# Positions loaded first, Pool's angle table ahead of the padding's memsets, powers between its steps, longer counted times for Pool

## Chip, core and metric

The kernel runs on one core of one Trainium2 chip. The time is device microseconds (us) of one execution. The core has a matrix engine (PE in the profile; its weight loads are PEld), a vector engine (DVE), a scalar engine (ACT), GpSimd (POOL) and a queue engine (SP) that issues DMA transfers; POOL can issue DMA transfers too, on a queue of its own. Each engine works off its own instructions in the order in which they were recorded, and waits where one of them needs what another engine or a transfer has not yet delivered.

## The reference

A two-layer decoder on 256 tokens of 1024 channels. Layer 0 has stick-breaking heads beside differential attention heads, layer 1 causal attention with 16 heads. The change concerns the way from the first norm to the rotated queries and keys:

```python
def rms_norm(x, g):
    y = xf * lax.rsqrt(jnp.mean(xf * xf, axis=-1, keepdims=True) + NORM_EPS)
    return y * g
def rope_tables(positions, head_dim):
    ang = positions.astype(jnp.float32)[..., None] * inv_freq     # (1, 256, 8)
    return jnp.cos(ang), jnp.sin(ang)
def apply_partial_rope(x, cos, sin):                              # of 64 channels of a head, 16 are turned
    r = jnp.concatenate([x1 * c - x2 * s, x1 * s + x2 * c], axis=-1)
# per layer:  h += mixer(rms_norm(h));  h += relu(rms_norm(h) @ w1)**2 @ w2
#             h += sigmoid(rms_norm(h) @ gate) * (p @ proj);        at the end rms_norm(h)
```

## The kernel before

All matrix products of the weights are made in three passes: a weight tile of 512 KB lands in one of four `raw` buffers, ACT rounds it to `whi`, DVE makes the rest `wlo = raw - whi`, and PE multiplies `whi` by the activations' high and low parts (`T0h`, `T0l`) and `wlo` by the high part (L159). Six pairs `whi`/`wlo` are in flight. In layer 0 the column blocks come in the order `bq`, `bk` (the differential heads' queries and keys), `aq`, `ak`, `av`, `bv`.

The order of instructions on each engine is made by a planner when the program is built (class `Order`). Tasks are generators; each yields the time or the event for which it waits, and of those that can go on the one of lowest rank goes on. `spend` adds a counted cost in ns to an engine's clock. The counted costs decide nothing on the chip but the order in which instructions stand. `o.idle(engine)` lets a task wait until the planner's clock of that engine has come by.

What the change touches:

- `table_task` makes the cosines and sines. POOL casts the positions (`posi` to `posf`), multiplies by the frequencies (`ang`) and takes multiples of 2 pi off in small steps (`prod`, `rem`; 16 elements a partition), ACT takes the sines, DVE makes `cc` and `sn`.
- `statistics` makes a norm's factor: ACT sums squares, DVE makes `ms_a`, POOL raises it to the power -0.5 (`rs_a`, L534), DVE makes an eighth of it for the queries (`rs8`, a part of the tile `rs_a`). There are two token tiles t, so two powers.
- `rows_task` has PE spread the two factors over a row (L159 `bank<-ident,rs_a`).
- `qk_sink` takes a finished block of queries or keys out of PSUM to `tok`, scaled, has POOL turn it by `cc` and `sn` (four instructions through `tt_pool`, L196: `rp`, `rp` twice, `tok`), and has PE transpose it (L170 `bank<-ident,tok`).
- `z_tile` has POOL write zeros into the halves of `z` and `zl` that pad the keys. `ple_projection` copies its products from PSUM to `pp`.

Of the kernel before, what the change touches and what calls it, by code (L numbers as in the profile page):

```python
# [9 lines left out]
F32 = mybir.dt.float32  # L10
F32R = mybir.dt.float32r
BF16 = mybir.dt.bfloat16
I32 = mybir.dt.int32
AF = mybir.ActivationFunctionType
ALU = mybir.AluOpType
AX = mybir.AxisListType

P = 128
# [22 lines left out]
def width(ap):  # L41
    n = 1
    for s in ap.shape[1:]:
        n *= int(s)
    return n
# [37 lines left out]
class Order:  # L83
# [110 lines left out]

    def tt_pool(self, out, a, b, op, dep=0.0):
        self.nc.gpsimd.tensor_tensor(out, a, b, op=op)  # L196
        return self.spend("pool", 145.0 + 2.15 * width(out), dep)

    def stt(self, out, a, s, b, op0, op1, dep=0.0):
        dep = max(dep, self.after(out, a, s, b))  # L200
# [27 lines left out]
def kernel(  # L228
# [6 lines left out]
    nc = tc.nc  # L235
    cst = ctx.enter_context(tc.tile_pool(name="cst", bufs=1))
# [5 lines left out]
    o = Order(nc)  # L242
# [18 lines left out]
    grow = big.take()  # L261
    grow_a, grow_b = grow[1][0:16, 0:P], grow[1][0:32, P:2 * P]
    nc.gpsimd.dma_start(grow_a, attn_norm.rearrange("i (k q) -> (i k) q", q=P))
    nc.scalar.preload_act_table_set("trig_and_small")
    o.spend("act", 1300)

    def load_x(t, cs=(0, 1)):
        for c in cs:
            nc.sync.dma_start(h[t][:, c * HALF:(c + 1) * HALF], x[0, t * P:(t + 1) * P, c * HALF:(c + 1) * HALF])
            o.clk["dma"] += 730  # L270
            x_ev[t][c].t = o.clk["dma"] + 1400
# [8 lines left out]
    one = cst.tile([P, 1], F32, name="one")  # L280
    nc.vector.memset(one, 1.0)
    junk = cst.tile([P, HALF], BF16, name="junk")
    posi = cst.tile([P, 2], I32, name="posi")
    lraw = [outs.take() for _ in range(4)]
    gsub = cst.tile([P, P], F32, name="gsub")
    invf = cst.tile([P, 8], F32, name="invf")
# [99 lines left out]
    def dma_task():  # L386
        for n, u in enumerate(units):
            if n == 2:
                load_x(1)
                nc.sync.dma_start(posi, positions[0].rearrange("(t q) -> q t", q=P))  # L390
            if n == 7:
                small_loads()
            yield lambda: None if not raws.free else 0.0
            t0 = min(f[0] for f in raws.free)
            u.raw = raws.take()
            s = max(o.clk["dma"], t0, o.now + 100)
            if n == 0:
                for a in range(2):
                    nc.sync.dma_start(u.raw[1][:, a * 512:(a + 1) * 512], u.src[:, a, :])
                    s = o.clk["dma"] = max(o.clk["dma"], s) + 730  # L400
                    u.raw_ev[a].t = s + 1300
                    if a == 0:
                        load_x(0, (1,))
                        s = o.clk["dma"]
            else:
                nc.sync.dma_start(u.raw[1].rearrange("q (a n) -> q a n", a=u.a), u.src)
                u.raw_ev[0].t = u.raw_ev[1].t = s + 1430 + 1300
                o.clk["dma"] = s + 1430
# [42 lines left out]
    def drop(u):  # L451
        splits.give(*u.buf, o.clk["pe"] + o.LAT)
        used[0] += 1
# [91 lines left out]
    def mm3(ps, ahi, alo, whi, wlo, start, stop):  # L545
        o.mm(ps, ahi, whi, start, False)
        o.mm(ps, ahi, wlo, False, False)
        return o.mm(ps, alo, whi, False, stop)
# [377 lines left out]
    def ple_projection(i, pT, pT_ev, st_ev, pps, pp_ev):  # L926
        yield st_ev
        pp = vpool.tile([P, 2, D], F32, tag="s", name=f"pp{i}")
        pps.append(pp)
        us = [units[pp_at[i]], units[pp_at[i] + 1]]  # L930
        w = 0.0
        for t in range(2):
            ts_ = slice(t * P, (t + 1) * P)
            for c in range(2):
                cs = slice(c * HALF, (c + 1) * HALF)
                bk = None
                for k in range(2):
                    yield (o.idle("pe"), us[k].ev[c], pT_ev)
                    if bk is None:
                        yield banks.wake  # L940
                        bk = banks.take()
                    mm3(bk[1], pT[:, 0, k, ts_], pT[:, 1, k, ts_], us[k].hi[:, 0, cs], us[k].lo[:, 0, cs], k == 0, k == 1)

                def evac(bk, t, cs, dep):
                    yield dep
                    e = o.copy(pp[:, t, cs], bk[1], ps=True)
                    banks.give(*bk, e)
                o.add(evac(bk, t, cs, o.clk["pe"] + o.LAT), 25)
        for u in us:
            drop(u)  # L950
        pp_ev.t = o.now
# [128 lines left out]


    def table_task():
        yield 9500.0
        posf = cst.tile([P, 2], F32, name="posf")
        ang = cst.tile([P, 2, 8], F32, name="ang")
        ka = cst.tile([P, 2, 8], F32, name="ka")
        kb = cst.tile([P, 2, 8], F32, name="kb")
        rem = cst.tile([P, 2, 8], F32, name="rem")
        aux = cst.tile([P, 2, 8], F32, name="aux")
        sh = cst.tile([P, 2, 8], F32, name="sh")  # L1090
        ch = cst.tile([P, 2, 8], F32, name="ch")
        for j in range(8):
            nc.gpsimd.memset(invf[:, j:j + 1], INV_FREQ[j])
        nc.gpsimd.tensor_copy(posf, posi)
        for t in range(2):
            nc.gpsimd.tensor_tensor(ang[:, t, :], invf, posf[:, t:t + 1].to_broadcast([P, 8]), op=ALU.mult)

        magic, inv, b14 = 1.5 * 2.0 ** 23, 1.0 / (2.0 * math.pi), 2.0 ** 14
        pt = two_pi_parts()
        prod = cst.tile([P, 2, 8], F32, name="prod")  # L1100

        def affine(dst, a, m, c):
            nc.gpsimd.tensor_scalar(dst, a, m, c, op0=ALU.mult, op1=ALU.add)

        def less(dst, k, c, src):
            nc.gpsimd.tensor_scalar(prod, k, -c, None, op0=ALU.mult)  # L1106
            nc.gpsimd.tensor_tensor(dst, prod, src, op=ALU.add)  # L1107

        affine(ka, ang, inv / b14, magic)
        nc.gpsimd.tensor_scalar(ka, ka, -magic, None, op0=ALU.add)  # L1110
        less(rem, ka, pt[0] * b14, ang)
        less(rem, ka, pt[1] * b14, rem)
        less(aux, ka, pt[2] * b14, rem)
        affine(kb, aux, inv, magic)
        nc.gpsimd.tensor_scalar(kb, kb, -magic, None, op0=ALU.add)
        for k, c in ((kb, pt[0]), (ka, pt[2] * b14), (kb, pt[1]), (ka, pt[3] * b14),
                     (kb, pt[2]), (ka, pt[4] * b14), (kb, pt[3]), (kb, pt[4])):
            less(rem, k, c, rem)
        e = o.spend("pool", 8700)
        yield e  # L1120

        o.act(sh, rem, AF.Sin, scale=0.5)
        e = o.act(aux, rem, AF.Abs, scale=0.5)
        yield e
        affine(aux, aux, -1.0, math.pi / 2)
        e = o.spend("pool", 200)
        yield e
        e = o.act(ch, aux, AF.Sin)
        nc.scalar.preload_act_table_set("natural_log_exp_and_others")
        o.spend("act", 1300)  # L1130
        yield e
        for t in range(2):
            o.stt(sn[:, t, 1, :], sh[:, t, :], 2.0, ch[:, t, :], ALU.mult, ALU.mult)
            o.ts(sn[:, t, 0, :], sn[:, t, 1, :], -1.0)
            o.stt(cc[:, t, 0, :], sh[:, t, :], -2.0, sh[:, t, :], ALU.mult, ALU.mult)
            o.ts(cc[:, t, 0, :], cc[:, t, 0, :], 1.0, None, ALU.add)
            e = o.ts(cc[:, t, 1, :], cc[:, t, 0, :], 1.0)
        rope_ev.t = e

        yield (28000.0, small_ev)  # L1140
        yield o.idle("dve")
        for j in range(2):
            a, b = lraw[2 * j][1], lraw[2 * j + 1][1]
            o.tt(a, a, b, ALU.mult)
            nc.vector.tensor_reduce(lsum[:, j], a.rearrange("q (h d) -> q h d", h=4), axis=AX.X, op=ALU.add)
            e = o.spend("dve", 340)
        for l_ in lraw:
            outs.give(*l_, e)
        yield e
        e = o.act(lsum, lsum, AF.Exp)  # L1150
        yield e
        o.tt(nlam, lsum[:, 0, :], lsum[:, 1, :], ALU.subtract)
        lam_ev.t = o.ts(nlam, nlam, LAM_INIT, -1.0, ALU.add, ALU.mult)
        o.ts(gsub, gsub, 1.0 - LAM_INIT)

    o.add(table_task(), 15)

    pT = cst.tile([P, 2, 2, 256], F32R, name="pT")

# [21 lines left out]
    def z_tile(name, layer, j):  # L1181

        z = zpool.tile([P, 4, 2, 256], F32R, tag="z", name=name)
        def zeros():
            yield o.now if layer else 1500.0
            for y in (z, zl[j]) if layer == 0 else (z,):
                nc.gpsimd.memset(y[64:128, :, 0, :].bitcast(F32), 0.0)  # L1187
                nc.gpsimd.memset(y[0:64, :, 1, :].bitcast(F32), 0.0)  # L1188
                o.spend("pool", 1800)
        o.add(zeros(), 14)  # L1190
        return z, zl[j]

    sl = [cst.tile([P, 4, 256], F32R, name=f"sl{j}") for j in range(2)]
# [98 lines left out]
```

## Time and profile before

| | us |
|---|---|
| median of 3 runs | 673.91 (673.76 to 673.92) |
| the profiled execution, its own time | 674.04 |
| its span on the core | 672.2 |
| PE busy | 654.2 (97%) |
| DVE, ACT busy | 451.6, 417.2 |
| POOL busy | 62.8 (9%) |

The span runs from the first to the last instruction that the profile recorded; the execution's own time has 1.84 us around it. A matmul's recorded end is modelled, and consecutive matmuls overlap in the records, so that a wait is longer than the idle time shown.

### The profile page before, as it was taken

What the parts mean: (1) busy time and instruction counts of PE and PEld (TensorE: products, weight loads), DVE (VectorE), ACT (ScalarE), POOL (GpSimd) and SP (SyncE); (2) the same over time, 40 slices, a digit from 0 to 9 for tenths busy, and PEclk for the clock granted to TensorE, in tenths of its full rate; (3) what the DMA queues carried; (4) which work ended last, traced back from release to release, by engine and by line L of the source; (5) the groups of instructions that cost most, each with busy time, mean ns of one, the idle gap of its engine ahead of it and who ended that gap; (6) DMA issues with size and microseconds to landing.
All of it is one profiled execution on the core that took longest, in us unless ns stands there. A gap on an engine that the chain in (4) does not pass through costs nothing.

```text
span 672.2 us, 10997 instructions
## 1 busy us (share of the span) xinstructions
PE 654.2 (97%) x3906; PEld 572.0 (85%) x3906; DVE 451.6 (67%) x936; ACT 417.2 (62%) x886; POOL 62.8 (9%) x129
## 2 busy tenths in 40 slices
PE   6799999999999999999999999999999999999995
PEld 5589878899998999898887878789998999899885
DVE  6789767677457555656995776758657545655594
ACT  6667887676446544655796776758646544655482
POOL 8820001000000000000043022000000000000010
PEclk9999999999999999999999999999999999999999
DMA  7662643456476446644556434525476546654621
GB/s 256 218 205 80 188 148 103 137 172 230 147 238 214 162 154 223 220 165 147 193 198 195 136 119 151 157 95 173 154 239 217 161 147 227 220 175 144 214 95 62
DMA packets 50055, 115.61 MB, mean 172 GB/s; under 512 B 4001, under 2 KB 5457, under 8 KB 50001
## 3 DMA queue, kind: packets, MB, share of 16 engines
q1 hardware_dynamic: 49824, 114.39, 52.1%
q8 instruction: 30, 0.49, 0.3%
q0 software_dynamic: 176, 0.53, 0.2%
q14 instruction: 25, 0.20, 0.1%
HBM read 113.86 MB, written 1.05 MB: 171 GB/s over the span
## 4 chain that ended last, share of the span: by engine, by line
PE 81%; issue 8%; POOL 8%; ACT 2%; DVE 0%; POOLq 0%; DVEq 0%; ACTq 0%
PE bank L159 78%; POOL rp L196 3%; PE bank L170 2%; POOL tok L196 1%; PE bank L165 1%; ACT tok L178 1%; POOL prod L1106 1%; POOL rem L1107 1%; ACT junk L178 0%; POOL zl L1187 0%; POOL z L1188 0%; POOL zl L1188 0%; POOL z L1187 0%; ACT whi L178 0%; ACT L1028 0%
## 5 line engine op out<-in xcount | busy, mean ns | idle before, releaser
L192 DVE TENSOR_TENSOR wlo<-raw,whi 128x512 fp32r<-128x512 f32 x424 | 276.7, 695 | 87.7 <-ACT whi L178 61.9
L178 ACT ACTIVATE whi<-raw 128x512 fp32r<-128x512 f32 x424 | 243.6, 628 | 96.1 <-PE bank L159 72.0
L159 PE MATMUL bank<-T0h,whi 128*128 128x256 f32 x576 | 162.4, 282 | 0.0
L159 PE MATMUL bank<-T0h,wlo 128*128 128x256 f32 x576 | 162.0, 281 | 0.0
L159 PE MATMUL bank<-T0l,whi 128*128 128x256 f32 x576 | 162.0, 281 | 0.0
L159 PE MATMUL bank<-whi,hid 128*128 128x512 f32 x512 | 161.0, 390 | 0.0
L159 PEld LDWEIGHTS bank<-whi,hid 128*128 128x128 f32 x512 | 96.1, 188 | 19.3
L159 PEld LDWEIGHTS bank<-T0h,wlo 128*128 128x128 f32 x576 | 110.5, 192 | 0.0
L159 PEld LDWEIGHTS bank<-T0l,whi 128*128 128x128 f32 x576 | 108.3, 188 | 0.7
L159 PEld LDWEIGHTS bank<-T0h,whi 128*128 128x128 f32 x576 | 108.3, 188 | 0.7
L159 PE MATMUL bank<-wlo,hid 128*128 128x512 f32 x256 | 99.6, 389 | 0.0
L192 DVE TENSOR_TENSOR tok<-tok 128x512 f32<-128x512 f32 x32 | 22.0, 689 | 66.9 <-ACT tok L178 66.9
L159 PE MATMUL bank<-whi,T0h 128*128 128x512 f32 x160 | 65.7, 411 | 0.8 <-DVE T0h L510 0.8
L159 PE MATMUL bank<-wlo,T0h 128*128 128x512 f32 x160 | 63.4, 396 | 0.0
L178 ACT ACTIVATE tok<-bank 128x512 f32<-128x512 f32 x32 | 18.8, 587 | 71.8 <-PE bank L159 71.8
L159 PE MATMUL bank<-whi,T0l 128*128 128x512 f32 x160 | 63.1, 394 | 0.0
L159 PEld LDWEIGHTS bank<-wlo,hid 128*128 128x128 f32 x256 | 48.1, 188 | 9.3
L159 PE MATMUL bank<-whi,T1h 128*128 128x512 f32 (+1 forms) x136 | 53.4, 393 | 0.0
L159 PE MATMUL bank<-whi,T1l 128*128 128x512 f32 (+1 forms) x136 | 51.5, 379 | 0.0
L159 PE MATMUL bank<-wlo,T1h 128*128 128x512 f32 (+1 forms) x136 | 51.4, 378 | 0.0
L534 POOL TENSOR_TENSOR rs_p<-ms_p,pexp 128x1 f32<-128x1 f32 x4 | 2.2, 554 | 434.4 <-DVE ms_p L209 434.4
L159 PEld LDWEIGHTS bank<-whi,T0h 128*128 128x128 f32 x160 | 30.5, 191 | 7.0 <-DVE T0h L510 1.2
(161 smaller groups left out, 740.5 us busy)
## 6 DMA issues: line engine op xcount, KB each, us to landing
raw<-in_w_ff_dram SPq DMA_DIRECT2D x128, 512.0 KB, 4.4
raw<-in_moba_w_in_dram SPq DMA_DIRECT2D x24, 512.0 KB, 4.2
raw<-in_ab_w_in_dram SPq DMA_DIRECT2D x23, 512.0 KB, 4.3
raw<-in_ple_gate_dram SPq DMA_DIRECT2D x16, 512.0 KB, 5.0
raw<-in_ab_w_out_dram SPq DMA_DIRECT2D x8, 512.0 KB, 4.6
raw<-in_moba_w_out_dram SPq DMA_DIRECT2D x8, 512.0 KB, 3.3
raw<-in_ple_proj_dram SPq DMA_DIRECT2D x4, 512.0 KB, 3.3
h<-in_x_dram SPq DMA_DIRECT2D x4, 256.0 KB, 5.2
```

The lines of the kernel that those rows point to most:

```text
L159: self.nc.tensor.matmul(out, lhsT, rhs, start=start, stop=stop, **kw)
L165: self.nc.tensor.matmul(out, lhsT, rhs, start=start, stop=stop)
L170: self.nc.tensor.transpose(out, in_, ident)
L178: self.nc.scalar.activation(out, in_, func, **kw)
L192: self.nc.vector.tensor_tensor(out, a, b, op=op)
L196: self.nc.gpsimd.tensor_tensor(out, a, b, op=op)
L534: nc.gpsimd.tensor_tensor(nm.rs[:, t:t + 1], b, pexp[:, 0:1], op=ALU.pow)
L1106: nc.gpsimd.tensor_scalar(prod, k, -c, None, op0=ALU.mult)
L1107: nc.gpsimd.tensor_tensor(dst, prod, src, op=ALU.add)
```

## The change

The positions are loaded by POOL's queue right behind the first norm's gains, and no longer by SP behind the first weights. The angle table may start at the planner's 1.0 us where it was 9.5, and its POOL steps are put one by one, so that other POOL work can stand between them; its last POOL step goes to DVE. The padding's memsets in layer 0 wait until the planner's 18 or 30 us and stand alone as well. A POOL instruction of the rotation is counted at 565 ns whatever its width. The copies to `pp` are all ACT's.

```diff
     def tt_pool(self, out, a, b, op, dep=0.0):
         self.nc.gpsimd.tensor_tensor(out, a, b, op=op)
-        return self.spend("pool", 145.0 + 2.15 * width(out), dep)
+        return self.spend("pool", 565.0, dep)
...
     nc.gpsimd.dma_start(grow_a, attn_norm.rearrange("i (k q) -> (i k) q", q=P))
+    posi = cst.tile([P, 2], I32, name="posi")
+    nc.gpsimd.dma_start(posi, positions[0].rearrange("(t q) -> q t", q=P))
...
                 load_x(1)
-                nc.sync.dma_start(posi, positions[0].rearrange("(t q) -> q t", q=P))
...
                     yield dep
-                    e = o.copy(pp[:, t, cs], bk[1], ps=True)
+                    yield o.idle("act")
+                    e = o.act(pp[:, t, cs], bk[1], AF.Copy, ps=True)
...
     def table_task():
-        yield 9500.0
+        yield 1000.0
...
+        o.clk["pool"] = 5000.0
+
         def affine(dst, a, m, c):
             nc.gpsimd.tensor_scalar(dst, a, m, c, op0=ALU.mult, op1=ALU.add)
+            return o.spend("pool", 420)
 
         def less(dst, k, c, src):
             nc.gpsimd.tensor_scalar(prod, k, -c, None, op0=ALU.mult)
             nc.gpsimd.tensor_tensor(dst, prod, src, op=ALU.add)
...
+            return o.spend("pool", 800)
...
         for k, c in ((kb, pt[0]), (ka, pt[2] * b14), (kb, pt[1]), (ka, pt[3] * b14),
                      (kb, pt[2]), (ka, pt[4] * b14), (kb, pt[3]), (kb, pt[4])):
-            less(rem, k, c, rem)
-        e = o.spend("pool", 8700)
+            yield o.idle("pool")
+            e = less(rem, k, c, rem)
         yield e
...
-        affine(aux, aux, -1.0, math.pi / 2)
-        e = o.spend("pool", 200)
+        e = o.ts(aux, aux, -1.0, math.pi / 2, ALU.mult, ALU.add)
...
-    o.add(table_task(), 15)
+    o.add(table_task(), 32)
...
         def zeros():
-            yield o.now if layer else 1500.0
+            yield o.now if layer else (18000.0 if j else 30000.0)
             for y in (z, zl[j]) if layer == 0 else (z,):
-                nc.gpsimd.memset(y[64:128, :, 0, :].bitcast(F32), 0.0)
-                nc.gpsimd.memset(y[0:64, :, 1, :].bitcast(F32), 0.0)
-                o.spend("pool", 1800)
-        o.add(zeros(), 14)
+                for rows, g in ((slice(64, 128), 0), (slice(0, 64), 1)):
+                    yield o.idle("pool")
+                    nc.gpsimd.memset(y[rows, :, g, :].bitcast(F32), 0.0)
+                    o.spend("pool", 980)
+        o.add(zeros(), 34)
```

POOL, at the end of the angle table in layer 0, before: all eight memsets stand ahead of the table, and both powers behind its last step.

```order
L1106 TENSOR_SCALAR prod<-kb 128x16
L1107 TENSOR_TENSOR rem<-prod,rem 128x16
L534 TENSOR_TENSOR rs_a_167<-ms_a_166,pexp 128x1 x2
L1103 TENSOR_SCALAR aux<-aux 128x16
L298 CAST identb<-ident 128x128
L299 MEMSET cmask 128x256
```

The same place now (L1110 and L1111 are the table's steps, L1197 the memsets of `z` and `zl`):

```order
L1111 TENSOR_TENSOR rem<-prod,rem 128x16
L534 TENSOR_TENSOR rs_a_167<-ms_a_166,pexp 128x1
L1110 TENSOR_SCALAR prod<-kb 128x16
L1111 TENSOR_TENSOR rem<-prod,rem 128x16
L1197 MEMSET z_169 64x4x256 x2
L1197 MEMSET zl_155 64x4x256
L299 CAST identb<-ident 128x128
L300 MEMSET cmask 128x256
```

The second power stands ahead of the table's last step. The first one stands six steps from the end (of the eight in the last loop, two are done). Three memsets have come between the table and the masks; a fourth stands behind the masks, two more between the second and the third rotation, and the last two behind the fourth.

DVE in the first block of `bq` (`wlo_86` and `wlo_88` are its third and fourth weight tiles):

```order
 L527 TENSOR_REDUCE ms_a_166<-ss_a_165 128x1
 L209 TENSOR_SCALAR ms_a_166<-ms_a_166 128x1
-L192 TENSOR_TENSOR wlo_86<-raw_79,whi_85 128x512 x2
-L192 TENSOR_TENSOR wlo_88<-raw_80,whi_87 128x512 x2
+L209 TENSOR_SCALAR rs_a_167<-rs_a_167 128x1
+L192 TENSOR_TENSOR wlo_86<-raw_79,whi_85 128x512 x2
+L192 TENSOR_TENSOR wlo_88<-raw_80,whi_87 128x512 x2
```

The eighth of the first factor, which needs POOL's first power, now stands ahead of these four halves; before, nineteen further instructions stood between.

PE at the spreading of the factors, before, in the first matmuls of `bk` (`whi_89`):

```order
L159 MATMUL bank_75<-whi_87,T0l 128x512
L159 MATMUL bank_76<-whi_89,T0h 128x512
L159 MATMUL bank_76<-wlo_90,T0h 128x512
L159 MATMUL bank_76<-whi_89,T0l 128x512
L159 MATMUL bank_69<-ident,rs_a_167 128x128 x2
L159 MATMUL bank_76<-whi_89,T0h 128x512
```

And now, in the second half of `bq`:

```order
L159 MATMUL bank_75<-whi_83,T0h 128x512
L159 MATMUL bank_75<-wlo_84,T0h 128x512
L159 MATMUL bank_75<-whi_83,T0l 128x512
L159 MATMUL bank_76<-ident,rs_a_167 128x128 x2
L159 MATMUL bank_75<-whi_83,T0h 128x512
```

The spreading has moved up by 18 matmuls. The transposes of the first rotated block (`tok_100`) have gone the other way, from 15 matmuls behind that place to 45 behind it, and those of the other three blocks, and of the blocks in layer 1 too, stand some matmuls later than before.

## Rows read from the trace of the kernel before

**Rows 1.** The page: the span and the engines' busy time.
```profile
span 672.2 us, 10997 instructions
...
PE 654.2 (97%) x3906; PEld 572.0 (85%) x3906; DVE 451.6 (67%) x936; ACT 417.2 (62%) x886; POOL 62.8 (9%) x129
```

**Rows 2.** PE's timeline, layer 0: start, length, line, operation; idle before, releaser.
```profile
22.78 0.39 PE L159 MATMUL bank<-wlo,T0h 128*128 128x512 f32 x1
23.01 0.39 PE L159 MATMUL bank<-whi,T0l 128*128 128x512 f32 x1
25.02 1.01 PE L159 MATMUL bank<-ident,rs_a 128*128 128x128 f32 x4 [1.62 <-POOL rs_a L534]
25.79 0.48 PE L159 MATMUL bank<-whi,T0h 128*128 128x512 f32 x1
...
30.84 0.66 PE L170 MATMUL bank<-ident,tok 128*128 128x128 f32 x4 [1.38 <-POOL tok L196]
...
33.70 0.66 PE L170 MATMUL bank<-ident,tok 128*128 128x128 f32 x4 [0.42 <-POOL tok L196]
...
42.18 0.66 PE L170 MATMUL bank<-ident,tok 128*128 128x128 f32 x4 [0.55 <-POOL tok L196]
...
44.14 0.66 PE L170 MATMUL bank<-ident,tok 128*128 128x128 f32 x4 [0.24 <-POOL tok L196]
```

**Rows 3.** PE's timeline, layer 1, the same columns.
```profile
368.76 0.66 PE L170 MATMUL bank<-ident,tok 128*128 128x128 f32 x4 [0.35 <-POOL tok L196]
...
414.74 0.66 PE L170 MATMUL bank<-ident,tok 128*128 128x128 f32 x4 [0.36 <-POOL tok L196]
```

**Rows 4.** POOL's timeline, the same columns.
```profile
1.32 0.66 POOL L263 DMA_DIRECT2D big<-in_attn_norm_dram  x1 [0.82 <-POOLq L1278]
...
9.64 0.95 POOL L1188 MEMSET zl<- 64x1024 f32 x1
...
10.81 0.43 POOL L1094 CAST posf<-posi 128x2 f32<-128x2 int32 x1
...
19.16 0.57 POOL L1106 TENSOR_SCALAR prod<-kb 128x16 f32<-128x16 f32 x1
...
24.39 1.09 POOL L534 TENSOR_TENSOR rs_a<-ms_a,pexp 128x1 f32<-128x1 f32 x2
...
28.08 0.40 POOL L312 CAST negr<-big 128x256 fp32r<-128x256 f32 x1
...
33.18 0.46 POOL L196 TENSOR_TENSOR tok<-rp 128x128 f32<-128x128 f32 x1
```

**Rows 5.** DMA issues: transfer, queue, count, size, us from issue to landing.
```profile
gB<-in_final_norm_dram POOLq DMA_DIRECT2D x1, 512.0 KB, 3.8
...
big<-in_attn_norm_dram POOLq DMA_DIRECT2D x1, 8.0 KB, 3.3
posi<-in_positions_dram SPq DMA_DIRECT2D x1, 1.0 KB, 6.6
```

**Rows 6.** POOL's timeline at the end: the issue of the other transfer on POOL's queue.
```profile
639.51 0.67 POOL L1258 DMA_DIRECT2D gB<-in_final_norm_dram  x1
```

**Rows 7.** DVE's timeline.
```profile
9.68 1.06 DVE L510 CAST T0h<-tok 128x256 fp32r<-128x256 f32 x1
...
12.33 0.28 DVE L510 CAST T0h<-tok 128x256 fp32r<-128x256 f32 x1
...
13.50 2.54 DVE L192 TENSOR_TENSOR wlo<-raw,whi 128x512 fp32r<-128x512 f32 x4 [0.18 <-ACT whi L178]
...
25.00 0.15 DVE L209 TENSOR_SCALAR rs_a<-rs_a 128x1 f32<-128x1 f32 x1 [2.92 <-POOL rs_a L534]
```

**Rows 8.** PE's timeline: its start, and the first block of `bq`.
```profile
4.78 0.25 PE L170 MATMUL bank<-ident,big 16*128 16x16 f32 x1 [4.78 <-DMA big<-in_attn_norm_dram]
...
9.16 0.63 PE L159 MATMUL bank<-whi,T0h 128*128 128x512 f32 x1
...
14.60 0.39 PE L159 MATMUL bank<-wlo,T0h 128*128 128x512 f32 x1
```

More of the change, by code (lines that the diff above doesn't have):

```diff
@@ L282 @@
     junk = cst.tile([P, HALF], BF16, name="junk")
-    posi = cst.tile([P, 2], I32, name="posi")
     lraw = [outs.take() for _ in range(4)]
@@ L1107, in less, with whole @@
             nc.gpsimd.tensor_tensor(dst, prod, src, op=ALU.add)
[L1109 to L1115, printed above, removed]
+            return o.spend("pool", 800)
+        def whole(dst, a, m):
+            affine(dst, a, m, magic)
+            nc.gpsimd.tensor_scalar(dst, dst, -magic, None, op0=ALU.add)
+            return o.spend("pool", 420)
+        whole(ka, ang, inv / b14)
+        for d_, k, c, v in ((rem, ka, pt[0] * b14, ang), (rem, ka, pt[1] * b14, rem), (aux, ka, pt[2] * b14, rem)):
+            yield o.idle("pool")
+            less(d_, k, c, v)
+        yield o.idle("pool")
+        whole(kb, aux, inv)
         for k, c in ((kb, pt[0]), (ka, pt[2] * b14), (kb, pt[1]), (ka, pt[3] * b14),
                      (kb, pt[2]), (ka, pt[4] * b14), (kb, pt[3]), (kb, pt[4])):
-            less(rem, k, c, rem)
-        e = o.spend("pool", 8700)
+            yield o.idle("pool")
+            e = less(rem, k, c, rem)
         yield e
@@ L1184, in zeros @@
         def zeros():
-            yield o.now if layer else 1500.0
+            yield o.now if layer else (18000.0 if j else 30000.0)
             for y in (z, zl[j]) if layer == 0 else (z,):
-                nc.gpsimd.memset(y[64:128, :, 0, :].bitcast(F32), 0.0)
-                nc.gpsimd.memset(y[0:64, :, 1, :].bitcast(F32), 0.0)
-                o.spend("pool", 1800)
-        o.add(zeros(), 14)
+                for rows, g in ((slice(64, 128), 0), (slice(0, 64), 1)):
+                    yield o.idle("pool")
+                    nc.gpsimd.memset(y[rows, :, g, :].bitcast(F32), 0.0)
+                    o.spend("pool", 980)
+        o.add(zeros(), 34)
         return z, zl[j]
```

## Prediction, made before the changed kernel was run

> **What bounds the kernel now.** I read the page first. PE is busy 654.2 of 672.2 us [rows 1], so only time in which PE stands still can be won, and the question is where it stands still and for whom. PE's list of waits and then its timeline answer that: after the start, every idle stretch before the tail ends on POOL. In layer 0 PE waits once for the powers (1.62 us idle before 25.02) and four times for rotated blocks (1.38, 0.42, 0.55 and 0.24) [rows 2]; in layer 1 twice more (0.35 and 0.36) [rows 3]. The reader is to see that the idle time understates the loss: consecutive matmuls start 0.23 apart but are recorded with 0.39, so 0.16 of each wait hides under the last record [rows 2]. Layer 0 loses 4.21 + 5 x 0.16 = 5.0 us, layer 1 0.71 + 2 x 0.16 = 1.0.
>
> POOL's timeline then says why it is late. It writes zeros until 10.59, starts on the angles at 10.81, reaches the two powers only at 24.39 and the masks' end at 28.48; it never pauses on that way [rows 4]. DVE shows the same delay from the other side: 2.92 us idle before the eighth of the first factor [rows 7].
>
> **The table starts earlier.** Now POOL issues two transfers, makes the identity, and waits for the positions. The issue begins where the first one ends, at 1.32 + 0.66 = 1.98 [rows 4]. No row shows the positions on POOL's queue. The bounds are 3.3 (the other early transfer of that queue) and 6.6 (the positions on SP's, behind the first weights) [rows 5]. I take 4.0, because the queue's own two transfers need 3.3 and 3.8 but this one consists of 256 pieces of four bytes. So the positions are there at L = 6.0 (bounds 5.3 and 8.6), 4.8 us before the cast at 10.81.
>
> Here the Trainium skill speaks against the change: "DMA: Bandwidth & Descriptors", Latency and other measured facts, gives the first byte some 0.4 us later on GpSimd's queue than on SP's. The two queues' rows here, 3.3 and 6.6, go the other way, since SP's transfer stood behind those of the first weights. By the page's figure alone the sum below would be an estimated 0.4 worse.
>
> **The powers between the steps.** From the cast to the step at 19.16, where the first power now stands, POOL needed 8.35 us, and a power takes 1.09 / 2 = 0.55 [rows 4]. The first power ends at L + 8.9 = 14.9. The remaining six steps took 24.39 - 19.16 = 5.23; five of them are 4.4, so the second power ends at 14.9 + 4.4 + 0.55 = 19.8 and the table at 20.7.
>
> **A new wait on DVE.** The eighth of the first factor stands ahead of `wlo_86` and `wlo_88`. DVE was free for the first of these at 13.50 [rows 7], and now stands until 14.9 + 0.06 (semaphore, from 24.94 to 25.00 [rows 4, 7]) + 0.15 for the eighth = 15.1. Then a half takes about 0.65 (2.54 / 4), and PE, which reached its first `wlo_86` matmul at 14.60 [rows 8], can only at 15.8. That is a new hold of PE of **1.2 us**, in a place where it waited for nobody. Queued behind it on DVE are the high and low parts of the second token tile's activations; in DVE's order they come within 0.65 each just ahead of PE, so they add nothing more. Generally the hold is L - 4.8: 0.5 at the early bound, 3.8 at the late one.
>
> **The spread factors.** PE comes to them 20 matmuls later, at 15.8 + 20 x 0.23 = 20.4; the second power is ready at 19.8. No wait, with 0.6 to spare.
>
> **The rotations.** After the table (20.7) POOL has three memsets at 0.95 [rows 4], the masks (25.48 to 28.48 before, 3.0 [rows 4]) and one more memset: 27.5. Then the rotations: two took from 28.48 to 33.64, 2.6 each [rows 4]. So the first block is ready at 30.1, the second at 32.7. PE comes to the first transposes 66 matmuls after the hold, with the spreading (0.77, from 25.02 to 25.79 [rows 2]) between: 15.8 + 66 x 0.23 + 0.8 = 31.8, and to the second nine matmuls and 0.4 later, at 34.3. Two memsets (1.9) are done by 34.6; the third block leaves PSUM 0.7 after PE's last matmul on it (35.0), is taken out in 0.7, rotated by 38.3 and the fourth by 40.9, while PE arrives at about 39.6 and 41.8. All four clear by 0.9 to 1.7. But POOL's steps vary: the same product took 0.57 here and 0.25 elsewhere in this table, and DVE is busier beside it now. I put **0.5** in for that (bounds 0 and 2).
>
> **Layer 1.** Two rotations back to back were counted 2.81 and take up to 5.2 in layer 0 [rows 4]; both waits fall on the second of such a pair [rows 3]. Counted at 2.26 each, the planner puts the second transposes six or more matmuls later, 1.4 us, against 0.5 of loss each. I take the whole **1.0** (bounds 0 and 1.0).
>
> **At nothing.** The last angle step on DVE instead of POOL: 0.15 like the eighth [rows 7], inside PE's matmuls of `bq`. The memsets moved: POOL has time, and the first reader of `z` comes after the fourth rotation; without that cover each costs 0.95. Two of the eight copies to `pp` change from DVE to ACT, under the first feed-forward matmuls; without that cover 0.6 each. SP loses one issue. Other order differences reach to the end of each layer's attention; the feed-forward and gate stages keep theirs.
>
> **The sum.** 5.0 - 1.2 - 0.5 + 1.0 = 4.3 us. The profiled execution took 674.04, 0.13 over the median, so 669.7 against it and **669.6** against the median of 673.91. Faster or slower by 0.2% means 1.35 us, about what a measurement of this kernel can tell from no change.
>
> **Rivals.**
>
> *POOL still ends last.* The memsets between the masks and the rotations and DVE's load beside POOL make the blocks late again. For it: POOL has no pause until 43; against it: the clearances above. If the steps take 2 us more than taken, the loss is 2.0 in place of 0.5: **671.1**. It decides from about 1.5 of delay.
>
> *The positions come late,* as on SP's queue: L = 8.6, the hold on DVE is 3.8. For it: weights and positions share the DMA engines at that time. Against it: the two rows of POOL's queue. 5.0 - 3.8 - 0.5 + 1.0 = 1.7: **672.2**.
>
> *The start gains too.* A cast on DVE took 1.06 at 9.68 beside a memset that began at 9.64, and 0.28 at 12.33 with no memset there [rows 4, 7]. With the memsets gone from the start, DVE is some 0.8 ahead for each such cast, but PE then waits for `wlo_86` just the same, unless the power comes early too (L = 5.3, hold 0.5, no delay of the rotations). Then PE gains 0.5 at the start: 674.0 - (5.0 - 0.5 + 1.0 + 0.5) = 668.0, at best **667.8**. The Trainium skill has the rule behind it ("SBUF — State Buffer", Who interferes with whom: VectorE, in some of its modes, and GpSimd share a port pair; the one that issues first holds it for its whole instruction, and the other waits). The trace agrees, with the 1.06 against 0.28.
>
> *The clock falls in the hold.* PE's first matmuls are recorded with 0.63 (9.16), later ones with 0.39 (14.60) [rows 8]: the lower and the upper of its two levels, 1.2 and 2.4 GHz. The hold comes right after that rise. If it costs the upper level once more, the stretch at the lower one lasts at most as long as at the start, 14.60 - 4.78 = 9.8, and takes back half, 4.9. Against it: after 1.62 idle at 25 the matmuls came back with 0.48 and not 0.63 [rows 2]. Result with a usual 4.0: **673.7**, no change.
>
> *The issue costs POOL time by the piece.* This one ends on the other side. The gains are 16 pieces and took POOL 0.66 [rows 4]; at the same rate 256 pieces take 10.6, and behind them stands the identity, without which PE's first transposes at 4.78 [rows 8] can't start. The identity would come at 13.1, PE 8.3 later; the hold grows to about 2.1. 674.0 + 8.3 - (5.0 - 2.1 - 0.5 + 1.0) = **678.9**. It decides from an issue of about 5 us on. Against it: the transfer of `gB`, of 128 rows, took POOL 0.67 [rows 6], no more than 16 pieces did.
>
> **Chances and range.** The forecast (668.2 to 670.6) 0.52; POOL last 0.20; late positions 0.12; the start too 0.06; the clock 0.05; by the piece 0.05. The range is to leave out no more than two in ten: from 667.6 (early positions and the start) to 672.6 (late positions and some delay of the rotations). Faster is all of the forecast, POOL last, the start and most of the late positions, 0.86; the same is the clock and the rest of these, 0.09; slower 0.05.
>
> **What would show it.** Right: POOL's cast of the positions near 6, the first power ending near 15, DVE idle ahead of the eighth of the first factor by one to two us and PE idle near 15 by about one, named as waiting for DVE; then no PE wait on POOL up to 45, and none near 368 and 414. Wrong: a cast after 8, PE waits on `tok` still there, first transposes after 4.8, matmuls recorded with 0.63 after 15, or new PE waits between 46 and 126, where the order differs and I have counted nothing.

## The result: slower, by a filler that moved and a start that did not keep its gain

The changed kernel took 678.41 us (median of four runs, 677.22 to 680.15) against 673.84 of the kernel before in the same comparison: 1.0069 times as long, with a 95% interval of 1.0057 to 1.0082. The prediction said 669.6, with a range of 667.6 to 672.6. The profiled execution took 677.22, with a span of 675.5, 3.3 us over that of before.

The page of the changed kernel, beside [rows 1]: span, busy time, and the engines' shares of the chain that ended last.

```profile
span 675.5 us, 10987 instructions
...
PE 654.2 (97%) x3906; PEld 571.6 (85%) x3906; DVE 449.3 (67%) x933; ACT 418.6 (62%) x890; POOL 63.3 (9%) x129
...
PE 90%; DVE 3%; DMA 2%; POOL 2%; issue 1%; ACT 1%; POOLq 0%; DVEq 0%; ACTq 0%
```

PE's busy time is the same 654.2, so by the page what was added is idle time, 21.3 us where it was 18.0 (a stretch at a lower clock counts as busy). POOL's share of the chain is 2% where it was 8%: the change did what it says, and the loss lies elsewhere. Where, shows when PE comes to the same instruction. All kernels here have 3906 of them on PE, counted from 0; the table gives the start of some in the profile of before, and how much later (+) or earlier the changed kernel and three experiments, told below, start the instruction of that number. Their orders differ by a few matmuls in places, so a tenth or two in a cell is nothing.

| PE instruction | before | changed | e5 filler last | e7 rotations first | e12 rotations first, filler early |
|---|---|---|---|---|---|
| 30, in `bq` | 14.60 | +1.62 | +1.69 | +0.04 | +0.53 |
| 140, before the third block | 41.35 | -2.68 | -2.62 | -3.92 | -3.48 |
| 200, behind the fourth | 49.66 | +0.44 | +0.41 | -5.13 | -4.69 |
| 600, before the output projection | 114.77 | +0.39 | +0.37 | -4.48 | -4.06 |
| 1200, in the feed-forward | 206.03 | +1.58 | +1.12 | -3.74 | -2.06 |
| 2000, before layer 1's attention | 342.52 | +1.58 | +1.12 | -3.74 | -2.06 |
| 2800, in layer 1's feed-forward | 484.62 | +3.23 | +1.00 | -3.85 | +0.28 |
| 3905, the last | 664.48 | +3.18 | +0.99 | -3.86 | +0.29 |

Read down the column of the changed kernel: 1.6 lost in the hold, 4.3 won by the powers and the first two blocks, 3.1 lost at the third block, 1.2 at the first feed-forward's start, 1.65 in layer 1. The sum is 3.2. The rows, in that order.

POOL's timeline of the changed kernel, beside [rows 4]:

```profile
1.98 0.78 POOL L265 DMA_DIRECT2D posi<-in_positions_dram  x1
...
8.21 0.22 POOL L1095 CAST posf<-posi 128x2 f32<-128x2 int32 x1 [4.58 <-DMA posi<-in_positions_dram]
...
14.77 0.57 POOL L534 TENSOR_TENSOR rs_a<-ms_a,pexp 128x1 f32<-128x1 f32 x1
...
33.21 0.79 POOL L196 TENSOR_TENSOR tok<-rp 128x128 f32<-128x128 f32 x1
...
39.35 0.91 POOL L196 TENSOR_TENSOR rp<-tok,cc 128x128 f32<-128x128 f32 x1 [3.34 <-ACT tok L178]
...
41.79 0.78 POOL L196 TENSOR_TENSOR tok<-rp 128x128 f32<-128x128 f32 x1
```

The positions came 6.2 us after their issue at 1.98, so L is 8.2. The issue itself took 0.78, so it did not cost POOL time by the piece. The table goes through without a pause, the first two blocks are turned by 34.0, and for the third POOL waits 3.34 us for ACT.

DVE's timeline at the hold, beside [rows 7]:

```profile
15.37 0.15 DVE L209 TENSOR_SCALAR rs_a<-rs_a 128x1 f32<-128x1 f32 x1 [2.44 <-POOL rs_a L534]
15.45 0.71 DVE L192 TENSOR_TENSOR wlo<-raw,whi 128x512 fp32r<-128x512 f32 x1
```

PE's timeline there, beside [rows 8], and at the places of [rows 2]:

```profile
13.94 0.44 PE L159 MATMUL bank<-whi,T0h 128*128 128x512 f32 x1
16.21 0.50 PE L159 MATMUL bank<-wlo,T0h 128*128 128x512 f32 x1 [1.84 <-DVE wlo L192]
...
20.88 0.61 PE L159 MATMUL bank<-ident,rs_a 128*128 128x128 f32 x4
...
31.97 0.60 PE L170 MATMUL bank<-ident,tok 128*128 128x128 f32 x4
...
34.48 0.60 PE L170 MATMUL bank<-ident,tok 128*128 128x128 f32 x4
...
40.00 0.39 PE L159 MATMUL bank<-T0h,wlo 128*128 128x256 f32 x1
42.62 0.67 PE L170 MATMUL bank<-ident,tok 128*128 128x128 f32 x4 [2.24 <-POOL tok L196]
...
43.52 0.41 PE L159 MATMUL bank<-T0h,wlo 128*128 128x256 f32 x1
```

DVE stands 2.44 us for the first power and PE behind it 1.84. The three waits on POOL of [rows 2] up to 34 are gone: no bracket at the spreading (20.88) and at the first two blocks (31.97, 34.48). The third block costs 2.24 by the bracket and 2.5 from start to start (40.00 to 42.62, less the usual 0.12), and the matmuls behind it are recorded with 0.41, where they have 0.28 elsewhere. The windows say what that is (engines' busy time with counts, then PE's granted clock, DMA share and GB/s):

```profile
43.10:46.50 3.40, 3.40 (x18) 3.40 (x17) 1.40 (x3) 1.19 (x2) 3.21 (x6) 0.51 0.85 290
46.60:50.00 3.40, 3.40 (x31) 3.40 (x30) 1.77 (x3) 2.22 (x4) 0.00 (x0) 1.00 0.24 85
```

The granted clock is 0.51 for this stretch, the lower of PE's two levels (1.2 GHz), and 1.00 behind it. What PE did before it fell: it stood for the third block. In the first of these windows PE did 18 matmuls, in the second 31 in the same time, so the lower clock cost about 1.4. ACT's timeline shows why that block came no earlier:

```profile
31.96 1.15 ACT L178 ACTIVATE whi<-raw 128x512 fp32r<-128x512 f32 x2 [1.44 <-DMA raw<-in_ab_w_in_dram]
34.20 0.63 ACT L178 ACTIVATE whi<-raw 128x512 fp32r<-128x512 f32 x1 [1.08 <-DMA raw<-in_ab_w_in_dram]
...
36.89 1.16 ACT L178 ACTIVATE whi<-raw 128x512 fp32r<-128x512 f32 x2 [1.05 <-DMA raw<-in_ab_w_in_dram]
...
38.52 1.26 ACT L178 ACTIVATE tok<-bank,rs_a 128x512 f32<-128x512 f32 x2
```

The same copy in the kernel before:

```profile
38.52 0.69 ACT L178 ACTIVATE tok<-bank,rs_a 128x512 f32<-128x512 f32 x1 [0.23 <-PE bank L159]
```

ACT takes the third block out of PSUM at 38.52 in both. Before, it had waited for PE; now it is behind three waits for weights in its order (1.44, 1.08, 1.05). PE is 2.7 us ahead (table) of a block that comes no earlier.

Last, a place that the prediction had left out, the start of the feed-forward. PE's timeline of the changed kernel in layer 0:

```profile
124.66 0.39 PE L159 MATMUL bank<-whi,pT 128*128 128x512 f32 x1
...
127.41 0.39 PE L159 MATMUL bank<-whi,pT 128*128 128x512 f32 x1
...
135.13 0.39 PE L159 MATMUL bank<-whi,T1l 128*128 128x512 f32 x1
...
138.30 0.39 PE L159 MATMUL bank<-whi,pT 128*128 128x512 f32 x1
138.53 0.60 PE L170 MATMUL bank<-ident,h 128*128 128x128 f32 x4
140.54 0.38 PE L159 MATMUL bank<-T0h,whi 128*128 128x256 f32 x1 [1.40 <-DVE T0h L510]
```

And in layer 1:

```profile
466.32 0.38 PE L159 MATMUL bank<-T0h,whi 128*128 128x256 f32 x1 [1.22 <-DVE T0h L510]
...
468.79 0.38 PE L159 MATMUL bank<-T0h,whi 128*128 128x256 f32 x1 [0.48 <-DVE T0h L510]
```

DVE's timeline of the changed kernel ahead of the first of these waits:

```profile
137.79 2.49 DVE L192 TENSOR_TENSOR wlo<-raw,whi 128x512 fp32r<-128x512 f32 x4
140.20 0.29 DVE L510 CAST T0h<-tok 128x256 fp32r<-128x256 f32 x1
```

PE of the kernel before, at the same place in layer 0:

```profile
132.01 0.39 PE L159 MATMUL bank<-whi,T1l 128*128 128x512 f32 x1
...
138.36 0.39 PE L159 MATMUL bank<-whi,pT 128*128 128x512 f32 x1
138.59 0.28 PE L159 MATMUL bank<-T0h,whi 128*128 128x256 f32 x1
```

The filler is work of the lowest rank, which the planner puts where PE would else stand: here the 24 matmuls on `pT` of `ple_projection` in each layer. In the kernel before, all 24 stood between the output projection's last matmul (132.01) and the feed-forward (138.59), and PE waited for nothing. Now twelve of them stand at 124.66 to 127.41, ahead of the projection's second half. What is left, twelve matmuls and two groups of transposes, keeps PE at work for 4.0 us from the last matmul of the projection (135.13) on, while the way through the residual, the transposes, ACT and DVE's cast to `T0h` at 140.20, behind four `wlo` halves, takes 5.4. In layer 1 nine of the 24 went ahead, and PE waits twice.

### The profile page after: what moved, and what is told of

Same layout as the page of the kernel before. It is cut to its first block, busy times and chain, and to the rows that moved or that the text cites. A ratio compares the mean times of both kernels' runs of the same rounds, so it can differ in the third digit from the quotient of the medians.

```text
span 675.5 us, 10987 instructions
## 1 busy us (share of the span) xinstructions
PE 654.2 (97%) x3906; PEld 571.6 (85%) x3906; DVE 449.3 (67%) x933; ACT 418.6 (62%) x890; POOL 63.3 (9%) x129
## 3 DMA queue, kind: packets, MB, share of 16 engines
HBM read 113.86 MB, written 1.05 MB: 170 GB/s over the span
## 4 chain that ended last, share of the span: by engine, by line
PE 90%; DVE 3%; DMA 2%; POOL 2%; issue 1%; ACT 1%; POOLq 0%; DVEq 0%; ACTq 0%
PE bank L159 86%; PE bank L170 3%; DVE wlo L192 2%; PE bank L165 1%; DMA posi<-in_positions_dram 1%; DMA raw<-in_ab_w_in_dram 1%; ACT tok L178 0%; DVE h L192 0%; POOL rp L196 0%; DVE T0l L192 0%; ACT whi L178 0%; DVE cc L209 0%; DVE T0h L510 0%; POOL prod L1110 0%; POOL rem L1111 0%
## 5 line engine op out<-in xcount | busy, mean ns | idle before, releaser
L159 PEld LDWEIGHTS bank<-wlo,T0h 128*128 128x128 f32 x160 | 30.5, 190 | 7.2 <-DVE wlo L192 2.1
```

The source lines that it names most:

```text
L159: self.nc.tensor.matmul(out, lhsT, rhs, start=start, stop=stop, **kw)
```

## The experiments

Theory F: the longer count of a POOL step makes the planner issue half of the filler early, and the feed-forward starts pay. Theory H: the hold makes the weights late, ACT with them, and so the third block; PE waits for it and its clock falls. Rival to F: the copies to `pp`, all on ACT, make the waits. Rival to H: the third block is late through POOL's own work. Each ratio is to the kernel before, with its 95% interval.

**Single parts of the change, on the kernel before.**

```diff
 e1:
-        return self.spend("pool", 145.0 + 2.15 * width(out), dep)
+        return self.spend("pool", 565.0, dep)
 e2:
-                    e = o.copy(pp[:, t, cs], bk[1], ps=True)
+                    yield o.idle("act")
+                    e = o.act(pp[:, t, cs], bk[1], AF.Copy, ps=True)
```

e1, the count alone. 

> The kernel before with one edit alone: a rotation step on Pool is counted 565 in the planner. Theory F (the longer count moves half of the filler matmuls on pT out of the end of the output projection, so that the feed-forward starts wait for the activations of the norm): PE loses 1.9 us at the start of layer 0's feed-forward and 2.4 to 2.7 at layer 1's, as in the changed kernel, and the 1.0 of layer 1's waits for rotated blocks is gone; layer 0's waits on Pool stay at about 5: 673.8 + 4.6 - 1.0 = 677.4. Rival (the copies of pp on ScalarE make those waits; the count only helps): no wait there, 672.8.

Measured: 676.04, 1.0035 (1.0023 to 1.0047). PE waits for `T0h` at both feed-forward starts, 1.38 and 1.81 us, with nothing else of the change there: F. The layer-0 waits on POOL are smaller than expected, because the count also moves the transposes of the first blocks back on PE, which the 677.4 had not allowed for. Behind the second of these waits the clock fell in the profiled execution (677.14, the longest of five). The window there:

```profile
465.80:469.10 3.30, 3.30 (x17) 3.30 (x17) 3.09 (x9) 0.71 (x3) 0.00 (x0) 0.50 0.73 238
```

e2, the copies alone. 

> The kernel before with one edit alone: all eight copies to pp on ScalarE. PE's order is that of before. Theory F: the filler still stands at the end of the output projection, no wait at either feed-forward start: 673.8 within 0.5. Rival (the copies on ScalarE make the waits): 673.8 + 4.6 = 678.4.

Measured: 673.95, 1.0000 (0.9991 to 1.0008). The rival to F falls, and the copies cost nothing.

**The old count in the changed kernel**, e3, which undoes e1's line. 

> The changed kernel with the old count of a rotation step; everything else of the change stays. Theory F: the waits at both feed-forward starts go (4.6), layer 1's two waits for rotated blocks come back (1.0): 678.4 - 4.6 + 1.0 = 674.8, with the hold of VectorE for the eighth and what follows it still there. Rival (the copies of pp make the waits): 678.4 or more.

Measured: 676.15, 1.0025 (1.0016 to 1.0034). No wait at either feed-forward start, and layer 1's two waits on POOL back. The hold (1.8), the third block (2.2) and the clock remain; in the profiled execution the clock fell behind the hold too (0.50 from 16.8 to 20.1), which the 674.8 had not in it.

**The eighth later**, e4, so that DVE does not stand for the power:

```diff
         if need == "eighth":
-            yield e
+            yield e + 2000.0
```

> The changed kernel with VectorE's step for the eighth put 2 us later in the plan, behind the four low parts wlo_86 and wlo_88, so that VectorE does not stand for the power. Theory H (the hold frees the raw buffers late, the next weights come late, ScalarE waits for them in its order ahead of the third block, PE waits for that block, and its clock falls after that wait): hold 2.05, third block 2.5 and the clock's 1.6 all go: 678.4 - 6.1 = 672.3. Rival (the third block's wait and the clock have other causes, such as later x or slower rotations): only the hold goes, 676.4, with the wait near 40 and the clock of 0.5 from 43 still there.

Measured: 678.45, 1.0059 (1.0039 to 1.0079): both missed. The hold went, and came back as a wait of 3.71 for the first block at 33.55, with the lower clock from its last part on (0.50 from 32.9 to 39.6). POOL says why; its timeline in this run:

```profile
15.51 1.02 POOL L534 TENSOR_TENSOR rs_a<-ms_a,pexp 128x1 f32<-128x1 f32 x1
...
30.30 0.89 POOL L196 TENSOR_TENSOR rp<-tok,cc 128x128 f32<-128x128 f32 x1
...
32.71 0.78 POOL L196 TENSOR_TENSOR tok<-rp 128x128 f32<-128x128 f32 x1
```

DVE's timeline in this run:

```profile
13.55 2.54 DVE L192 TENSOR_TENSOR wlo<-raw,whi 128x512 fp32r<-128x512 f32 x4 [0.94 <-ACT whi L178]
...
27.30 5.88 DVE L192 TENSOR_TENSOR wlo<-raw,whi 128x512 fp32r<-128x512 f32 x8
```

Here the power takes 1.02, with DVE's `wlo` passes beside it; at 14.77 in the changed kernel, with DVE idle, it took 0.57. The masks take 4.0 instead of 2.7 and the first rotation 3.2 instead of 2.4, and the first block is ready at 33.5 where it was at 30.8. For the power, DVE's standing had been what made POOL fast. Beside most of the masks and the rotation DVE now has eight `wlo` halves in a row; in the changed kernel its next row of them began at 29.07, behind the masks. The Trainium skill has a rule for that ("SBUF — State Buffer", Who interferes with whom): a VectorE instruction with two SBUF inputs, as this subtraction is, contends with a GpSimd instruction that reads SBUF. The trace agrees, with 1.02 against 0.57 for the power.

**The filler last**, e5 on the changed kernel and e6 on the kernel before with e1's count:

```diff
-            o.add(ple_projection(i, pT, pT_ev, st_ev, pp, pp_ev), FILL)
 ...
             yield from out_proj(oacts, nm)
+            o.add(ple_projection(i, pT, pT_ev, st_ev, pp, pp_ev), FILL)
```

> The changed kernel with one edit: the filler matmuls on pT may only be issued once the output projection has been issued, so all 24 stand again between its last matmul and the feed-forward. Theory F: no wait at either feed-forward start; the clock does not fall there; the hold, the third block's wait and the clock near 43 stay, and layer 1 keeps its gain of 1.0: 678.4 - 3.9 = 674.5. Rival (the waits there come from the norm's own chain being late, whatever stands ahead): waits of over 1 us stay, 678.

Measured: 675.83, 1.0023 (1.0014 to 1.0033). The waits for `T0h` of 1.40, 1.22 and 0.48 are gone, as F says. New ones stand in both layers ahead of the projection's second half, where the early filler had been: PE waits 0.5 twice for ACT's `T1h`. So in this order the filler covers one of two places, and the feed-forward is the dearer one. The kernel before, and e3, wait at neither with all the filler last: in layer 0 their last transposes ahead of this place stand nine matmuls earlier on PE (number 637, here 646). More had moved than the filler.

> The kernel before with the longer count of a rotation step and the filler held behind the output projection; nothing of the table, the positions or the memsets. Theory F: the feed-forward starts lose nothing, layer 1's waits for rotated blocks are gone: 676.0 - 3.9 = 672.1. Rival (the count has other costs): 674 or more.

Measured: 672.87, 0.9982 (0.9973 to 0.9992). Without table, positions or memsets, the count brings 1.2 once its filler is held, and little of it in layer 1: from instruction 2000 to 2800 PE gains 0.20.

**The rotations first**, e7: e5 and e4 together, and POOL's masks and memsets behind the first two rotations.

```diff
-        yield (20000.0, big.wake)
+        yield (30000.0, big.wake)
 ...
-            yield o.now if layer else (18000.0 if j else 30000.0)
+            yield o.now if layer else (29000.0 if j else 45000.0)
```

> The changed kernel with the filler held behind the output projection, the eighth 2 us later in the plan, and Pool's masks and memsets behind the first two rotations. Theory P (with VectorE at work beside it Pool's table takes longer, and what stands between table and rotations made the first block late): the first block is ready near 30 or 31, PE waits for it under 1 us, the clock stays up, the third block does not make PE wait: 674.5 - 6 = 668.5. Rival (Pool is still late, or the third block waits as before): 671 or more.

Measured: 670.43, 0.9946 (0.9933 to 0.9959), the fastest of all. PE's timeline at the first and third block:

```profile
30.04 0.60 PE L170 MATMUL bank<-ident,tok 128*128 128x128 f32 x4
...
40.43 0.60 PE L170 MATMUL bank<-ident,tok 128*128 128x128 f32 x4
```

POOL's timeline, the first power and the rotations:

```profile
15.85 1.02 POOL L534 TENSOR_TENSOR rs_a<-ms_a,pexp 128x1 f32<-128x1 f32 x1
...
25.85 0.46 POOL L196 TENSOR_TENSOR rp<-tok,cc 128x128 f32<-128x128 f32 x1 [2.19 <-DVE sn L201]
...
30.22 0.79 POOL L196 TENSOR_TENSOR tok<-rp 128x128 f32<-128x128 f32 x1
...
38.98 0.79 POOL L196 TENSOR_TENSOR tok<-rp 128x128 f32<-128x128 f32 x1
```

The power is as slow as in e4, but nothing stands between table and rotations any more: both blocks are turned by 31.0, at 30.04 PE waits for nothing, and the third block comes at 39.8, ahead of PE at 40.43. The windows from 36 to 48 show a granted clock of 1.00. Theory P of the expectation held, with 1.9 less gain than hoped.

**The same with the hold**, e8: e7 without e4's line. 

> As the run with the rotations first, but with the eighth where the change has it, so that VectorE stands for the first power. Theory H (the hold makes the weights late, and so ScalarE, the third block and PE): the hold of 2.0 and the wait near 40 for the third block stay: 674.5. Rival (the third block was late through Pool's own work): the wait near 40 goes, 672 or less.

Measured: 671.83, 0.9975 (0.9965 to 0.9985), so the wait near 40 went, against H as I had put it. H's first half, that the hold makes the weights late, is shown by the changed kernel and e4, which differ in the eighth alone. SP's weight transfer behind the hold, in the changed kernel:

```profile
16.81 0.37 SPq L406 DMA_DIRECT2D raw<-in_ab_w_in_dram  x1
```

The same transfer in e4, without the hold:

```profile
14.89 0.37 SPq L406 DMA_DIRECT2D raw<-in_ab_w_in_dram  x1
```

ACT's copy of the third block, in e7:

```profile
36.14 1.25 ACT L178 ACTIVATE tok<-bank,rs_a 128x512 f32<-128x512 f32 x2
```

And ACT's copy in e8:

```profile
38.01 1.25 ACT L178 ACTIVATE tok<-bank,rs_a 128x512 f32<-128x512 f32 x2
```

PE's timeline in e8, at its start:

```profile
9.04 1.11 PE L170 MATMUL bank<-ident,h 128*128 128x128 f32 x4 [2.77 <-DMA h<-in_x_dram]
```

The hold makes the transfer 1.9 late. The copy is 1.87 later in e8 than in e7, but this can't be put down to the hold: in this execution of e8 a part of the input x landed late, PE stood 2.77 for it, and DVE then stood only 1.21 for the power where it stood 2.44 in the changed kernel. In e5, with x on time as in e7, the copy stands at 38.65, but e5 differs from e7 in POOL's order too. Why e8 does not wait for the third block can be added up: the planner puts its transposes behind 15 more matmuls (number 165 on PE instead of 150, 1.8 us at 0.12 each), and the block is ready 0.7 earlier than in the changed kernel (41.88 for 42.57). PE comes at 41.97.

**The small transfers later**, e9, on e5: SP's seven small loads behind the eleventh weight unit and not the seventh.

```diff
-            if n == 7:
+            if n == 11:
                 small_loads()
```

> The changed kernel with the filler held behind the output projection, and SP's seven small transfers (lambda, subln, the two gains) issued four weight units later, so that the next weights go out some 3.3 us earlier while VectorE still stands for the power. Theory H (the hold makes the weights late, ScalarE waits for them ahead of the third block, and PE for the block): ScalarE's waits for raw weights between 31 and 37 shrink from 3.6 to under 1, the third block is ready before PE comes, its wait of 2.5 and the clock's fall behind it go; the hold stays: 675.8 - 2.5 - 0.9 = 672.4. Rival (the third block is late for another reason): wait near 40 as before, 675.8.

Measured: 672.02, 0.9975 (0.9966 to 0.9984): the number that H gave, and no wait near 40. But not by H's way. In the profiled run ACT still waits for weights (1.11, and now 2.50 behind the small loads) and copies the block at 38.30, hardly earlier than 38.65 in e5; POOL turns it in 2.2 us instead of 3.2, and PE is 1.9 later, mostly because the clock fell in the hold of this execution (0.50 from 17.4 to 20.7). What the third block did in executions without that fall, no trace shows.

**The positions back on SP**, e10, on e5: the load behind the first weights, as before the change. 

> The changed kernel with the filler held behind the output projection, and the positions back on SP's queue behind the first weights; table and order as in the change. If the early issue on Pool's queue is what brings the positions at 8.2: they now land near 10, the first power near 17, VectorE stands 2 us longer and PE's hold grows from 2.1 to about 4: 675.8 + 2 = 677.8, or 1.7 more if the clock falls in the hold. Rival (the positions are bound by the same transfer engines on either queue): they land near 8.5, 676.

Measured: 677.70, 1.0049 (1.0037 to 1.0061), 1.9 over e5. The cast starts at 10.79, and PE stands 3.34 in the hold instead of 1.83, with the clock down in and behind it (0.50 from 16.5 to 23.3).

**The old count on e7**, e11: e3's edit; the later memsets also wait for the planner's 38 us and not 45, so this run differs from e7 in two things. 

> The run with the rotations first, with the old count of a rotation step. Theory F says the longer count is worth little by itself once the filler stands last (0.15 in layer 1, where its waits for rotated blocks only become other waits, and the third and fourth blocks of layer 0): the first block is asked for seven matmuls earlier, 1.6 us, which costs up to 1.5 there: 670.4 to 672.2. Rival (the count is worth the 1.0 of layer 1 in full, with waits of 0.5 there again): 671.4 plus what layer 0 costs, 673.

Measured: 671.09, 0.9957 (0.9945 to 0.9969), 0.66 over e7. The waits on POOL are back, four with 1.5 in all, two of them layer 1's. Yet from 2000 to 2800 this run gains 0.35 on the kernel before, and e7, without those waits, 0.11; e7 has a wait of 0.48 for `T1h` there (2548 on PE), and e11 has none.

**The filler early again on e7**, e12: without the edit of e5. 

> The run with the rotations first, without the edit on the filler: the start of that run, the feed-forward starts of the change. Theory F says that the two faults are separate places and add: the profile's ledger puts the feed-forward starts at 3.6, so 670.4 + 3.6 = 674.0, with the waits of 1.6, 1.4 and 0.6 there and none on Pool at the start; by the medians of the changed kernel with and without the filler edit (678.4 and 675.8) it is 673.0. Rival (the waits at the feed-forward come from PE being late or early against the other engines after the start): they change by over a half, and the time is outside 672.5 to 675.5.

Measured: 674.56, 1.0006 (0.9997 to 1.0015), 4.1 over e7 (4.2 in the profiled executions, where 0.4 of it lies at the start), with the waits of the changed kernel to within 0.02 (1.40, 1.21 and 0.47; there 1.40, 1.22 and 0.48). The two faults are separate, and either alone takes back all that e7 wins (the start 5.4, from e5 to e7).

## Why the prediction was wrong, step by step

- **Order differences "at nothing"**: the step that failed first. I wrote that the feed-forward stages keep their order and counted nothing. They do keep it; what had moved was their cover, and no rival of mine had that in it. It cost 2.6 (678.41 to 675.83, e5) in the changed kernel and 4.1 (e12 to e7) beside a good start. e1, e3 and e5 show the count as the cause and the filler's place as the way.
- **Layer 1, "the whole 1.0"**: mis-sized. Its waits on POOL did go, but with the filler last PE gains only 0.1 to 0.2 there (e5, e7, e6), and 0.35 with the old count (e11). Taking two waits of 0.5 away bought an order that costs nearly as much elsewhere; 0.48 of that is the new wait for `T1h`.
- **The new hold**: the mechanism was right, L was 8.2 and not 6.0. I had trusted POOL's other transfers; the positions took 5.2 to 7.0 in nine profiled executions on POOL's queue and 6.1 to 6.6 in five on SP's. The Trainium skill's difference of 0.4 between the queues ("DMA: Bandwidth & Descriptors", Latency and other measured facts) does not stand out of that spread. By my own formula the hold would be 3.4; it was 2.0 (13.94 to 16.21, less the usual 0.23), since POOL was faster, 7.1 from the cast to the first power's end and not 8.9, mostly in the steps while DVE stood. Net of a better start PE lost 1.6, and 1.2 was forecast. The early issue was still worth 1.9 (e10).
- **Powers and first two blocks**: right. No wait at the spreading and at the first two blocks, 4.3 won between instructions 30 and 140.
- **The third block, one of "All four clear" (ready at 38.3, PE there at 39.6)**: failed. I placed it by PE's last matmul on it. It hangs on ACT's copy, which stands in order behind weights, and ACT was there at 38.52 in both kernels. PE lost 2.5 instead of winning 0.7, and the clock took about 1.4 more; against that stand the 1.1 of the old waits for the third and fourth block, which makes most of the 3.1 in the table. That the hold makes the weights late is shown by the changed kernel against e4 (1.9), and that ACT stands for weights ahead of its copy by its rows. That the hold's lateness alone made PE wait is not shown: e8 has the copy nearly as late (38.01) and does not wait, and e9 removes the wait with the copy at 38.30. What stays open is how much of the 2.5 is the late weights and how much PE's order and POOL's slower turn.
- **Copies to `pp`**: nothing, as said (e2). **The memsets moved**: not nothing. Four of 0.95 still stood ahead of the rotations, and the masks. In the changed kernel they did no harm; without the hold, with PE earlier and POOL slower, they made the first block 3.7 late (e4), and with them and the masks behind the rotations it came in time (e7).
- **The clock**: given 0.05 and put in the hold. It fell behind the third block, in the profiled executions of e3, e9 and e10 behind the hold, and in e1's behind the feed-forward's wait in layer 1. The median is 1.2 above the profiled execution; whether more such stretches make that up, no trace shows.

## What to carry to other kernels

When a planner's counted costs change, look for filler work that has left its place, at every place in the program and not only near the change: work without a deadline is often the cover of a wait that no profile shows as long as it is covered. Where a wait is taken out, ask what the block hangs on next, by the row that writes it (here ACT behind weights) and not by the one that is waiting. And a helper engine's speed depends on what runs beside it: POOL's first power took 0.57 with DVE idle, and 1.02 beside DVE's passes.

## What the runs showed of the hardware

The clock fell to its lower level behind waits of PE that the trace records with 2.24 (the third block), 1.83 (the hold, in e3), 1.85 (the powers, in e2) and 1.81 (layer 1's feed-forward, in e1). It did not behind 1.84 in the changed kernel's own hold, nor behind 1.85 at the powers in e6 or 1.62 at the powers before. The Trainium skill ("TensorE: Matmul & The Clock Gate", Why this matters for your kernels) too names gaps between matmuls as what brings it down; in kind, these rows agree. Where PE is about to wait anyway it costs nothing: e2 had it, and took 673.72. The windows of e2 behind its wait:

```profile
26.10:29.40 3.30, 3.30 (x9) 2.62 (x8) 2.23 (x13) 3.29 (x6) 3.22 (x10) 0.50 0.58 179
29.50:33.00 3.50, 3.48 (x17) 2.23 (x15) 3.50 (x5) 2.90 (x8) 3.34 (x6) 1.00 0.41 130
```

And PE's spacing is not one number even at the upper level. Behind the wait at 140.54 the changed kernel ran the same feed-forward matmuls closer together than e12 did behind an equal wait, 166 in 18.5 us against 163 in 18.9, and won 0.7 back by 161; no run here shows why. The windows of the changed kernel:

```profile
141.50:160.00 18.50, 18.50 (x166) 18.50 (x165) 13.09 (x26) 10.55 (x20) 0.00 (x0) 1.00 0.63 207
```

And of e12:

```profile
137.10:156.00 18.90, 18.90 (x163) 18.90 (x162) 13.02 (x26) 10.48 (x20) 0.00 (x0) 1.00 0.62 207
```
